# A clock for SyncE's queue in the planner, and the ends of six HGRN heads turned by 32x32 blocks

## The chip, the core and the metric

The kernel runs on one core of one Trainium2 chip. The core's engines are TensorE (PE in the rows, with its weight loads as PEld), VectorE (DVE), ScalarE (ACT), GpSimd (POOL) and SyncE (SP), which issues nearly all DMAs. The metric is the device time of one execution in microseconds (us), the median of several runs.

## The reference, cut to what matters

One layer of a streaming encoder over 512 frames of 2048 features in float32. One input projection feeds two groups of heads, their gated outputs go through one output projection, and the result is normalised with the residual:

```
proj = x @ w_in                          # 512 x 2048 by 2048 x 8320
o_rwkv = rwkv7(proj[:4224]) * silu(z_r)  # 16 heads of 64: scan over chunks of 64 frames
o_hgrn = hgrn2(proj[4224:]) * silu(z_h)  # 8 heads of 128: gated linear recurrence, RMS norm
y = concat(o_rwkv, o_hgrn) @ w_out       # 512 x 2048 by 2048 x 2048
out = layer_norm(2 ** 0.25 * x + y)
```

What the change touches is the end of an HGRN head: its output of 512 frames by 128 values is divided by its root mean square over the values, and multiplied by a weight for each value and by silu(z):

```
o = o * rsqrt(mean(o * o, -1) + 1e-5)
o = o * g_norm_w * silu(z)
```

## The kernel before, in words

**Tiles.** Activations lie with 128 features on the partitions and 512 frames along the row. Each float32 product of the two projections is made of three products of halves (`xh`, `xl` of the activations, `wh`, `wl` of the weights, in the type float32r); the helper `three` issues them. Weights come in pieces of 128x1024 (`wr`, two buffers, 512 KB each, helper `load`), and each piece is split in two parts of 512 columns by ScalarE (`wh`, three buffers) and VectorE (`wl`, three buffers). A part feeds 12 products.

**Order of the work.** The input projection is a list of units of 128 columns (`_order`), 48 products each, which write one of four PSUM banks `main`. Between those products a planner (class `Plan`) puts everything else: for four groups of two pairs of RWKV heads the preparation (`rwkv_prep`), the inversion and the scan (`rwkv_invert`, `rwkv_scan`), the finish (`rwkv_finish`); for four groups of two HGRN heads `hgrn_heads`, which ends in `hgrn_out` for each head. These are generators in queues. The planner has a clock for each engine, a cost for each operation, and for each tile the times at which it is ready and free. After each product of a projection it goes round the queues and issues what its clocks allow: an operation for TensorE only when its inputs are ready 0.35 us ahead of TensorE's clock (`LEAD`), one for another engine when it would start soon (`SLACK`, `EARLY`). So the costs and due times in the planner decide the order in which instructions stand on each engine; on the chip each engine works its list through in order and waits on semaphores.

**Modes of TensorE.** The planner tells three kinds of product apart: *main* (float32r, 512 columns), *whole* (float32, 128x128) and *narrow* (fewer than 128 rows or columns). In what follows a *visit* is a run of whole or narrow products between two main ones.

**Turning a tile.** A head's values come out of its products with frames on the partitions, but the gated output `g` needs values on the partitions. In `hgrn_out` four products with the identity matrix (helper `tr`, one for each 128 frames) turn `o2` into a PSUM tile `pn`, which VectorE then multiplies with the weight and `S["g"]` (helper `stt`, into `g`). A second way exists already in the helper `turned`, which `rwkv_prep` uses for `bk` and `v`: VectorE turns each 32x32 block in place (`dtr`), and 16 DMAs (8 for `v`) from SBUF to SBUF, all from SyncE, carry the blocks to where they belong. In `turned` the planner holds 0.4 us for each DMA of a row of blocks, and takes the result as ready 3 us after the last hold.

**SyncE's queue.** Weights, the finished outputs `g` that are put away to DRAM and brought back (`spill`), the residual and the result are all issued from SyncE, in order. The planner before has a clock for DMA transfers (`fetched`) that starts from TensorE's clock; time that SyncE needs to issue is not in it. The finishes of RWKV pairs stand in one queue, `finishes`, one after the other.

**The out projection.** After the last unit its 16 inputs (`korder`: pairs 0 to 5, heads 0 to 5, then head 6, pair 6, head 7, pair 7) are split as the weights are, one step ahead of use, by `split_gated`. For the first quarter of the columns the 16 inputs are used in that order, 12 products each.

Of the kernel before, what the change touches and what calls it, by code (L numbers as in the profile page):

```python
# [15 lines left out]
P = 128  # L16
T = 512
D = 2048
# [44 lines left out]
class Plan:  # L63
# [15 lines left out]
    def __init__(self, room):  # L79
        self.clock = {"pe": 0.0, "dve": 0.0, "act": 0.0, "pool": 0.0, "dma": 0.0}  # L80
# [65 lines left out]
    def fetched(self, tile, size):  # L146

        self.clock["dma"] = max(self.clock["dma"], self.clock["pe"]) + size * 128 / 360e3
        self.ready[tile.tensor.name] = (self.clock["dma"] + 2.0, "dma")
# [92 lines left out]
def mixer_kernel(ctx, tc, head, x_r, w_all, par, up, ln_wb, consts, hmask, out):  # L242
# [64 lines left out]


# [83 lines left out]
    def turned(dst, src, tmp, rows=4, base=0):  # L392


        name = dst.tensor.name
        yield dtr(tmp, src)
        yield lambda: by_now(tmp)
        for a in range(4):
            for b in range(rows):
                o = base + 32 * b  # L400
                nc.sync.dma_start(dst[o : o + 32, :, 32 * a : 32 * a + 32],
                                  tmp[32 * a : 32 * a + 32, :, 32 * b : 32 * b + 32])
            at = plan.clock["pe"] + 0.4 * rows
            yield lambda: plan.clock["pe"] >= at
        plan.ready[name] = (plan.clock["pe"] + 3.0, "dma")
# [21 lines left out]
    def load(j):  # L427
        if j < nload:
            raws[j] = st("wr", [P, HALF])
            nc.sync.dma_start(raws[j], w_all[j - nhead])  # L430
# [117 lines left out]
    def constants():  # L548
        raw = st("ksq", [P, T])[:, : 16 * len(LEVELS)]
        for t, a in ((pr, par), (cst, consts), (raw, hmask)):  # L550
            nc.sync.dma_start(t, a)
# [48 lines left out]
    def put_gated(k, g):  # L600

        gated[k] = g
        if k in SPILL:
            def run():
                yield lambda: by_now(g)
                nc.sync.dma_start(spill[SPILL.index(k)], g)
# [8 lines left out]
    def next_up():  # L615
        if len(ups) < NPAIR:
            upw = take("up", [P, 2, P])
            nc.sync.dma_start(upw, up[len(ups)])
# [311 lines left out]
    def rwkv_group(SS, grp):  # L930
# [4 lines left out]
        def run():  # L935
# [3 lines left out]
            for i, S in enumerate(SS):  # L939
                plan.add(finishes, rwkv_finish(S, 2 * grp + i))  # L940
# [116 lines left out]
    def hgrn_out(S, h, q, k, dt_, dg, tot, tots):  # L1057
# [38 lines left out]
        yield landed(o2)  # L1096
        pn = take("mix")
        for j in range(4):
            yield tr(pn[:, j * P : j * P + P], o2[:, j * P : j * P + P])
        yield has(S, "g")  # L1100
        yield stt(g, pn, hcol(HHW, h), S["g"], ALU.mult, ALU.mult)
        drop(S["g"], pn, o2)
# [30 lines left out]
    groups, finishes, preps = plan.queue(), plan.queue(), plan.queue()  # L1133
# [14 lines left out]
    def fetch(k):  # L1148
        raw = firsts[k] = take("q4", [P, T + FIRST * P])
        if k:  # L1150
            nc.sync.dma_start(raw, head[k])
        else:

            nc.scalar.dma_start(raw[:, T:], head[k, :, T:])
            for c in (slice(0, T // 2), slice(T // 2, T)):
                nc.sync.dma_start(raw[:, c], head[k, :, c])
# [91 lines left out]
    def reload(n):  # L1248
        while len(asked) < min(n, KT):
            k = korder[len(asked)]  # L1250
            asked.append(k)
            if k in SPILL:
                plan.until(lambda: gated[k] is not None and (plan.free("t") or plan.free("g")))
                gated[k] = take("t" if plan.free("t") else "g")
                nc.sync.dma_start(gated[k], spill[SPILL.index(k)])
# [105 lines left out]
    def finish(t):  # L1361
# [4 lines left out]
        def norm():  # L1366
            ahead = []
            for d in range(5):
# [5 lines left out]
                if d:  # L1374
                    y, b, o, k = ahead.pop(0)
                    yield keyed(tt(y, y, b, ALU.add), k, k)
                    nc.sync.dma_start(o, y)
# [9 lines left out]
    def finish_last(t, pbs, weigh):  # L1387
# [16 lines left out]
        def norm():  # L1404
# [8 lines left out]
            for d in range(4):  # L1413
# [3 lines left out]
                for c in (slice(0, T),) if d < 3 else (slice(0, T // 2), slice(T // 2, T)):  # L1417
# [7 lines left out]
                    nc.sync.dma_start(o[:, c], y[:, c])  # L1425
# [27 lines left out]
    def residual(t, d):  # L1453
        plan.until(room(g=1))
        xrs[t] = take("g")
        nc.sync.dma_start(xrs[t], x_r[t, :, d * T : d * T + T])
# [9 lines left out]
    def ahead(j, d):  # L1466

        if d == 0:
            split_gated(j + 2)
            if j == 8:  # L1470
                plan.until(room(big=1))
                lnw.append(take("big", [P, 2, D]))
                nc.sync.dma_start(lnw[0], ln_wb[None].to_broadcast([P, 2, D]))
# [193 lines left out]
```

## Time and profile before

| | us |
|---|---|
| median of 3 runs (1050.09 to 1050.93) | 1050.35 |
| the profiled execution | 1050.24 |
| its span in the profile, first instruction to last | 1048.5 |

The profiled execution's own time and its span differ by 1.7 us, which lie outside the instructions. A difference in span is taken as a difference in time. The clock granted to TensorE over the span is 0.999 of full speed, that is the 2.4 GHz level.

### The profile page before, as it was taken

What the parts mean: (1) busy time and instruction counts of PE and PEld (TensorE: products, weight loads), DVE (VectorE), ACT (ScalarE), POOL (GpSimd) and SP (SyncE); (2) the same over time, 40 slices, a digit from 0 to 9 for tenths busy, and PEclk for the clock granted to TensorE, in tenths of its full rate; (3) what the DMA queues carried; (4) which work ended last, traced back from release to release, by engine and by line L of the source; (5) the groups of instructions that cost most, each with busy time, mean ns of one, the idle gap of its engine ahead of it and who ended that gap; (6) DMA issues with size and microseconds to landing.
All of it is one profiled execution on the core that took longest, in us unless ns stands there. A gap on an engine that the chain in (4) does not pass through costs nothing.

```text
span 1048.5 us, 18840 instructions
## 1 busy us (share of the span) xinstructions
PE 1040.6 (99%) x7342; PEld 865.1 (83%) x7342; DVE 755.7 (72%) x1653; ACT 437.6 (42%) x867; POOL 38.3 (4%) x81
## 2 busy tenths in 40 slices
PE   9999999999999999999999999999999999999997
PEld 8888888888888888888888888888888888888885
DVE  7465898667759987676689866865998778625556
ACT  6545333445353354452533353525334554323321
POOL 0000000000000000000000000000000002000000
PEclk9999999999999999999999999999999999999999
DMA  8134342222343522223534323234352244545613
GB/s 332 54 103 114 99 109 86 86 79 81 84 123 100 122 82 74 78 98 79 138 78 118 98 62 96 70 96 110 100 128 72 69 164 131 182 131 159 202 60 131
DMA packets 87305, 114.79 MB, mean 109 GB/s; under 512 B 56368, under 2 KB 58160, under 8 KB 87088
## 3 DMA queue, kind: packets, MB, share of 16 engines
q1 hardware_dynamic: 87072, 113.39, 36.6%
q8 instruction: 58, 0.95, 0.4%
q14 instruction: 31, 0.25, 0.1%
q10 hardware_dynamic: 144, 0.20, 0.1%
HBM read 99.92 MB, written 7.34 MB: 102 GB/s over the span
## 4 chain that ended last, share of the span: by engine, by line
PE 99%; DVE 1%; DVEq 0%; issue 0%
PE main L453 74%; PE mix L324 11%; PE mix L453 8%; PE main L1192 3%; PE main L324 2%; PE mix L328 1%; PE mix L1142 0%; DVE inv L356 0%; DVE inv L347 0%; DVE stats L1549 0%; DVEq L1663 0%; DVE mv L1357 0%; DVE bd L356 0%; DVE mv L352 0%; DVE inv L1140 0%
## 5 line engine op out<-in xcount | busy, mean ns | idle before, releaser
L453 PE MATMUL main<-xl,wh 128*128 128x512 f32 x864 | 341.1, 395 | 0.0
L453 PE MATMUL main<-xh,wl 128*128 128x512 f32 x864 | 341.1, 395 | 0.0
L453 PE MATMUL main<-xh,wh 128*128 128x512 f32 x864 | 340.9, 395 | 0.0
L337 ACT ACTIVATE wh<-wr 128x512 fp32r<-128x512 f32 x299 | 186.9, 627 | 237.1 <-PE main L453 180.5
L347 DVE TENSOR_TENSOR wl<-wr,wh 128x512 fp32r<-128x512 f32 x299 | 203.8, 682 | 61.8 <-ACT wh L337 60.1
L453 PEld LDWEIGHTS main<-xh,wh 128*128 128x128 f32 x864 | 162.4, 188 | 33.0
L453 PEld LDWEIGHTS main<-xh,wl 128*128 128x128 f32 x864 | 162.5, 188 | 32.6
L453 PEld LDWEIGHTS main<-xl,wh 128*128 128x128 f32 x864 | 162.4, 188 | 32.6
L453 PE MATMUL main<-wl,xh 128*128 128x512 f32 (+1 forms) x262 | 102.6, 392 | 0.0
L453 PE MATMUL main<-wh,xh 128*128 128x512 f32 (+1 forms) x262 | 102.1, 390 | 0.0
L453 PE MATMUL main<-wh,xl 128*128 128x512 f32 (+1 forms) x262 | 101.6, 388 | 0.0
L453 PEld LDWEIGHTS main<-wh,xh 128*128 128x128 f32 x262 | 49.2, 188 | 9.9
L453 PEld LDWEIGHTS main<-wh,xl 128*128 128x128 f32 x262 | 49.2, 188 | 9.7
L453 PEld LDWEIGHTS main<-wl,xh 128*128 128x128 f32 x262 | 49.2, 188 | 9.6
L338 ACT ACTIVATE t<-main,om 128x512 f32<-128x512 f32 x33 | 22.4, 687 | 51.1 <-PE main L453 41.6
L356 DVE SCALAR_TENSOR_TENSOR t<-main,pr,t 128x511 f32<-128x511 f32 x33 | 24.4, 747 | 26.5 <-ACT t L338 26.2
L347 DVE TENSOR_TENSOR inv<-inv,inv 64x30 f32<-64x30 f32 (+14 forms) x120 | 38.6, 322 | 2.9
L347 DVE TENSOR_TENSOR inv<-inv 64x30 f32<-64x30 f32 (+14 forms) x120 | 38.4, 320 | 2.3
L347 DVE TENSOR_TENSOR t<-t,tot 128x256 f32<-128x256 f32 x96 | 37.8, 414 | 1.8 <-PE mix L324 1.7
L356 DVE SCALAR_TENSOR_TENSOR bd<-mix,pc,bd 64x64 f32<-64x64 f32 x112 | 31.7, 283 | 7.5 <-PE mix L324 5.2
L337 ACT ACTIVATE zz<-mix 64x64 f32<-64x64 f32 x63 | 13.8, 220 | 46.9 <-PE mix L324 45.8
L338 ACT ACTIVATE t<-main 128x512 f32<-128x512 f32 x32 | 18.5, 598 | 30.7 <-PE main L453 30.2
(222 smaller groups left out, 1328.0 us busy)
## 6 DMA issues: line engine op xcount, KB each, us to landing
wr<-w_all SPq DMA_DIRECT2D x156, 512.0 KB, 3.6
q<-head SPq DMA_DIRECT2D x15, 448.0 KB, 5.9
q<-q SPq DMA_DIRECT2D x128, 32.0 KB, 2.4
g<-x_r SPq DMA_DIRECT2D x16, 256.0 KB, 3.8
spill<-g SPq DMA_DIRECT2D x12, 256.0 KB, 2.7
out<-q SPq DMA_DIRECT2D x12, 256.0 KB, 2.4
t<-spill SPq DMA_DIRECT2D x10, 256.0 KB, 4.2
zz<-ksq SPq DMA_DIRECT2D x64, 32.0 KB, 2.6
```

The lines of the kernel that those rows point to most:

```text
L324: return Op([("pe", cost, lambda: pe.matmul(o, l, r, start=start, stop=stop, **kw))], [l, r], [o], mode="narrow" if narrow else "main" if ...
L328: return Op([("pe", 0.11, lambda: pe.transpose(o, i, ident))], [i], [o])
L337: return "act", cost, lambda: sc_e.activation(o, i, f, scale=scale)
L338: return "act", cost, lambda: sc_e.activation(o, i, f, scale=scale, bias=bias)
L347: return dve_op([a, b], o, lambda: dve.tensor_tensor(o, a, b, f), base=0.16 if o.shape[0] < P and size(o) == C and o.tensor.name in tags e ...
L356: return dve_op([a, b], o, lambda: dve.scalar_tensor_tensor(o, a, s, b, f1, f2), per=0.00113, base=0.085 if o.shape[0] == P else 0.25 if s ...
L453: pe.matmul(ps, l, r, start=first and i == 0, stop=last and i == 2)
L1192: pe.matmul(pss[a], *ops, start=k == 0 and low == of == 0, stop=k == KT - 1 and low == 1)
```

## The change

The planner gets a clock `sp` for SyncE's queue. A new helper `send` issues a DMA and moves that clock on by 0.44 us, or by the cost given; all DMAs from SyncE go through it now. `fetched` starts a transfer from this clock and takes it as landed 1.8 us after its end, where it was 2.0. `turned` no longer holds 0.4 us for each block: it sends a block (0.65 us each) when SyncE's clock is at most 0.2 us ahead of TensorE's, and takes the tile as ready 2.6 us after the last one; it also keeps the source tile busy until then. In `hgrn_out` heads 0 to 5 use `turned` in place of the four products `tr`; heads 6 and 7 keep them. The multiplication that follows then reads `o2` in SBUF where it read `pn` in PSUM. The finishes of the two pairs of a group stand in two queues, not in one.

```diff
@@ -77,7 +77,7 @@
     EARLY = 0.5
 
     def __init__(self, room):
-        self.clock = {"pe": 0.0, "dve": 0.0, "act": 0.0, "pool": 0.0, "dma": 0.0}
+        self.clock = {"pe": 0.0, "dve": 0.0, "act": 0.0, "pool": 0.0, "sp": 0.0, "dma": 0.0}
         self.table = None
         self.mode, self.rest = "main", 0.0
         self.queues, self.waiting, self.hurry = [], {}, False
@@ -145,8 +145,8 @@
 
     def fetched(self, tile, size):
 
-        self.clock["dma"] = max(self.clock["dma"], self.clock["pe"]) + size * 128 / 360e3
-        self.ready[tile.tensor.name] = (self.clock["dma"] + 2.0, "dma")
+        self.clock["dma"] = max(self.clock["dma"], self.clock["sp"]) + size * 128 / 360e3
+        self.ready[tile.tensor.name] = (self.clock["dma"] + 1.8, "dma")
 
     def queue(self):
         self.queues.append([])
@@ -305,6 +305,11 @@
 
         return test
 
+    def send(o, i, cost=0.44):
+
+        nc.sync.dma_start(o, i)
+        plan.clock["sp"] = max(plan.clock["sp"], plan.clock["pe"]) + cost
+
 
     def size(ap):
         n = 1
@@ -397,12 +402,11 @@
         yield lambda: by_now(tmp)
         for a in range(4):
             for b in range(rows):
+                yield lambda: plan.clock["sp"] <= plan.clock["pe"] + 0.2
                 o = base + 32 * b
-                nc.sync.dma_start(dst[o : o + 32, :, 32 * a : 32 * a + 32],
-                                  tmp[32 * a : 32 * a + 32, :, 32 * b : 32 * b + 32])
-            at = plan.clock["pe"] + 0.4 * rows
-            yield lambda: plan.clock["pe"] >= at
-        plan.ready[name] = (plan.clock["pe"] + 3.0, "dma")
+                send(dst[o : o + 32, :, 32 * a : 32 * a + 32],
+                     tmp[32 * a : 32 * a + 32, :, 32 * b : 32 * b + 32], 0.65)
+        plan.ready[name] = plan.busy[tmp.tensor.name] = (plan.clock["sp"] + 2.6, "dma")
@@ -427,7 +431,7 @@
     def load(j):
         if j < nload:
             raws[j] = st("wr", [P, HALF])
-            nc.sync.dma_start(raws[j], w_all[j - nhead])
+            send(raws[j], w_all[j - nhead])
             plan.fetched(raws[j], 4 * HALF)
 
     whole_parts = set()
...
@@ -937,7 +941,7 @@
             yield from outputs(SS, sc)
             drop(sc)
             for i, S in enumerate(SS):
-                plan.add(finishes, rwkv_finish(S, 2 * grp + i))
+                plan.add(finishes[i], rwkv_finish(S, 2 * grp + i))
 
         plan.add(scans[0], run())
@@ -1093,13 +1097,19 @@
         yield tt(tiles(o2), tiles(po), rs[:, :, None].to_broadcast([P, 4, P]))
         drop(po, k, dt_, rs)
         S["used"]()
-        yield landed(o2)
-        pn = take("mix")
-        for j in range(4):
-            yield tr(pn[:, j * P : j * P + P], o2[:, j * P : j * P + P])
+        if h < 6:
+            yield from turned(tiles(o2), tiles(o2), tiles(g))
+            pn = o2
+        else:
+            yield landed(o2)
+            pn = take("mix")
+            for j in range(4):
+                yield tr(pn[:, j * P : j * P + P], o2[:, j * P : j * P + P])
         yield has(S, "g")
         yield stt(g, pn, hcol(HHW, h), S["g"], ALU.mult, ALU.mult)
-        drop(S["g"], pn, o2)
+        if h >= 6:
+            drop(pn)
+        drop(S["g"], o2)
         put_gated(8 + h, g)
 
     def silu2(ps, put):
@@ -1130,7 +1140,7 @@
 
 
     scans = [plan.queue(), plan.queue()]
-    groups, finishes, preps = plan.queue(), plan.queue(), plan.queue()
+    groups, finishes, preps = plan.queue(), [plan.queue(), plan.queue()], plan.queue()
     heads, stores = plan.queue(), plan.queue()
...
```

In the rest of the diff, from `constants` and `put_gated` to the loads at the end, `nc.sync.dma_start(o, i)` becomes `send(o, i)` and nothing else.

What this does to the order of instructions is read from the built programs. In all, TensorE has the same products as before but for 24 `tr` fewer, VectorE has six STREAM_TRANSPOSE of 128x512 more, and SyncE has 96 DMAs of 32x4x32 more. The lists are the same up to product 354 of TensorE (of 5697), and again for the last 626 products of TensorE, the last 133 operations of VectorE and the last 70 DMAs of SyncE; in between everything is shifted. TensorE leaves the main products 31 times for narrow ones, where it was 30, and has 117 runs of whole products, where it was 119.

First place, TensorE at the end of HGRN head 0 (`t_971` is its `o2`, `t_1292` the next head's `k`; `zz`, `q` belong to the RWKV scan). Before:

```order
L453 MATMUL main_2152<-xl_91,wh_2130 128x512
L328 MATMUL mix_2199<-cst,t_971 128x128 x4
L328 MATMUL mix_2209<-cst,t_1292 128x128 x3
L324 MATMUL mix_2214<-zz_832,q_447 128x128
L324 MATMUL mix_2215<-zz_1231,q_885 128x128
L453 MATMUL main_2152<-xh_75,wl_2131 128x512
```

Now, at the next head's `k` (`t_1259`); head 0's own four products are nowhere on TensorE:

```order
L457 MATMUL main_2397<-xh_74,wl_2375 128x512
L333 MATMUL mix_2443<-cst,t_1259 128x128 x3
L329 MATMUL mix_2457<-ksq_2418,ones_r 128x512
L329 MATMUL mix_2457<-ksq_2419,ones_r 128x512
L457 MATMUL main_2397<-xh_75,wh_2374 128x512
```

The four products of `o2` are gone from a visit that stays, with other neighbours. The six sets of four that go all stood, as here, in a visit with other whole products.

Second place, SyncE and VectorE for the same head. SyncE before, from the piece of weights ahead of head 0's spill:

```order
L430 DMA wr_2189<-w_all 128x1024
L606 DMA spill<-g_2080 128x512
L430 DMA wr_2277<-w_all 128x1024
L430 DMA wr_2356<-w_all 128x1024
L618 DMA up_2367<-up 128x256
```

SyncE now (`t_954` is head 0's `o2`, `g_2150` its `g`):

```order
L310 DMA wr_2297<-w_all 128x1024
L310 DMA up_2306<-up 128x256
L310 DMA t_954<-g_2150 32x4x32 x11
L310 DMA wr_2379<-w_all 128x1024
L310 DMA t_954<-g_2150 32x4x32 x5
L310 DMA wr_2451<-w_all 128x1024
L310 DMA spill<-g_2150 128x512
```

The 16 blocks stand between pieces of weights, with one piece amid them. In the other five heads the blocks stand 9 and 7, 6 and 10, 4 and 10 and 2, 11 and 5, 9 and 7 around such pieces. VectorE now, from the multiplication that makes `g` (the 23rd row after the block transposes of `t_954`):

```order
L371 STREAM_TRANSPOSE g_2150<-t_954 128x512
...
L361 SCALAR_TENSOR_TENSOR bd_1985<-mix_2411,pc_1040,bd_1985 64x64
L361 SCALAR_TENSOR_TENSOR g_2150<-t_954,half,t_2084 128x512
L352 TENSOR_TENSOR wl_2445<-wr_2297,wh_2444 128x512
L357 TENSOR_SCALAR ksq_2460<-mix_2457 128x512
L361 SCALAR_TENSOR_TENSOR rt_1986<-mix_2463,zz_872 64x128
L361 SCALAR_TENSOR_TENSOR rt_1987<-mix_2470,zz_1315 64x128
```

The multiplication now waits for 16 DMAs rather than for TensorE, and a split of weights (`wl`) and the next step of the scan (`rt`) stand behind it.

Third place, VectorE at the last input of the out projection, the finish of RWKV pair 7 (`mix_9487` and `mix_9368` hold its turned output). Before:

```order
L356 SCALAR_TENSOR_TENSOR g_9348<-mix_9368,half,t_7437 128x512
L356 SCALAR_TENSOR_TENSOR t_8898<-ksq_9349,t_8898 128x512
L356 SCALAR_TENSOR_TENSOR g_9348<-g_9348,half,t_8898 128x512
L347 TENSOR_TENSOR wl_9383<-wr_9273,wh_9382 128x512
L347 TENSOR_TENSOR xl_9395<-g_9227,xh_9394 128x512
L347 TENSOR_TENSOR wl_9407<-wr_9323,wh_9406 128x512
L347 TENSOR_TENSOR xl_9417<-g_9155,xh_9416 128x512
L347 TENSOR_TENSOR wl_9429<-wr_9323,wh_9428 128x512
L347 TENSOR_TENSOR xl_9441<-g_9348,xh_9440 128x512
```

Now:

```order
L361 SCALAR_TENSOR_TENSOR g_9467<-mix_9487,half,t_7489 128x512
L361 SCALAR_TENSOR_TENSOR t_8945<-ksq_9468,t_8945 128x512
L352 TENSOR_TENSOR wl_9500<-wr_9385,wh_9499 128x512
L361 SCALAR_TENSOR_TENSOR g_9467<-g_9467,half,t_8945 128x512
L352 TENSOR_TENSOR xl_9513<-g_9467,xh_9512 128x512
```

The finish has moved towards its use: on TensorE 47 main products stood between the four `tr` of pair 7 and the first product that reads its split, and now 22 do.

## Rows read from the trace of the kernel before

**Rows 1.** The page: busy time by engine, and the granted clock in 40 slices.
```profile
PE 1040.6 (99%) x7342; PEld 865.1 (83%) x7342; DVE 755.7 (72%) x1653; ACT 437.6 (42%) x867; POOL 38.3 (4%) x81
...
PEclk9999999999999999999999999999999999999999
```

**Rows 2.** All waits of PE: engine, line, releaser, us in total, times, longest.
```profile
PE mix L324 <- ACT ksq L1409: 1.5, 1, 1.5
PE mix L1142 <- DVE inv L1140: 1.1, 1, 1.1
PE mix L324 <- DVE bd L356: 0.4, 1, 0.4
```

**Rows 3.** Timeline of PE, a visit with seven `tr`: start us, us, instruction, count.
```profile
206.70 0.39 PE L453 MATMUL main<-xl,wh 128*128 128x512 f32 x1
206.93 0.93 PE L328 MATMUL mix<-cst,t 128*128 128x128 f32 x7
207.69 0.61 PE L324 MATMUL mix<-zz,q 128*128 128x128 f32 x4
208.06 0.48 PE L453 MATMUL main<-xh,wl 128*128 128x512 f32 x1
208.38 0.39 PE L453 MATMUL main<-xh,wh 128*128 128x512 f32 x1
208.61 0.39 PE L453 MATMUL main<-xl,wh 128*128 128x512 f32 x1
```

**Rows 4.** Groups by line: all `tr`, with busy us and mean ns of one.
```profile
L328 PE MATMUL mix<-cst,t 128*128 128x128 f32 x88 | 12.9, 273 | 0.0
```

**Rows 5.** Timeline of PE, around a visit of narrow products.
```profile
156.85 0.39 PE L453 MATMUL main<-wh,xh 128*128 128x512 f32 x1
157.17 0.70 PE L324 MATMUL mix<-t 128*32 128x16 f32 x62
...
158.37 0.50 PE L453 MATMUL main<-wl,xh 128*128 128x512 f32 x1
158.71 0.39 PE L453 MATMUL main<-wh,xl 128*128 128x512 f32 x1
```

**Rows 6.** Timeline of SyncE's queue, six blocks of `turned` one after the other.
```profile
130.44 3.86 SPq L401 DMA_DIRECT2D zz<-ksq  x6
```

**Rows 7.** Line L401, the blocks of `turned`: ns min/median/max to issue, us from issue to landing.
```profile
L401 SPq DMA_DIRECT2D q<-q x128: 585/608/1292, 74.9 to 768.5; - x128
...
DMA to landing us min/median/max: 1.9/2.5/4.8
```

**Rows 8.** Groups by line: VectorE's block transposes of one 128x512 tile.
```profile
L366 DVE STREAM_TRANSPOSE ksq<-t 128x512 f32<-128x512 f32 x8 | 5.6, 701 | 0.0
```

**Rows 9.** Timeline of all engines at a burst of spill loads, idle time in brackets.
```profile
837.32 1.81 SPq L1255 DMA_DIRECT2D t<-spill  x4
...
841.54 0.63 ACT L337 ACTIVATE xh<-t 128x512 fp32r<-128x512 f32 x1 [2.81 <-DMA t<-spill]
...
842.21 0.69 DVE L347 TENSOR_TENSOR xl<-t,xh 128x512 fp32r<-128x512 f32 x1 [1.76 <-ACT xh L337]
...
845.38 0.39 PE L453 MATMUL main<-xh,wh 128*128 128x512 f32 x1
...
846.03 0.29 DVE L356 SCALAR_TENSOR_TENSOR bd<-mix,pc,bd 64x64 f32<-64x64 f32 x1
...
846.93 0.39 PE L453 MATMUL main<-xh,wl 128*128 128x512 f32 x1
```

**Rows 10.** Timeline of PE and VectorE after the four `tr` of pair 6.
```profile
880.58 0.48 PE L453 MATMUL main<-wh,xl 128*128 128x512 f32 x1
...
880.87 0.75 DVE L356 SCALAR_TENSOR_TENSOR g<-mix,half,t 128x512 f32<-128x512 f32 x1 [1.35 <-PE mix L328]
881.53 0.68 DVE L356 SCALAR_TENSOR_TENSOR t<-ksq,t 128x512 f32<-128x512 f32 x1
882.13 0.68 DVE L360 TENSOR_REDUCE rs<-t 128x4 f32<-128x512 f32 x1
```

More of the change, by code (lines that the diff above doesn't have):

```diff
@@ L550, in constants @@
         for t, a in ((pr, par), (cst, consts), (raw, hmask)):
-            nc.sync.dma_start(t, a)
+            send(t, a)
             plan.fetched(t, 4 * size(t))
@@ L605, in run @@
                 yield lambda: by_now(g)
-                nc.sync.dma_start(spill[SPILL.index(k)], g)
+                send(spill[SPILL.index(k)], g)
                 drop(g)
@@ L617, in next_up @@
             upw = take("up", [P, 2, P])
-            nc.sync.dma_start(upw, up[len(ups)])
+            send(upw, up[len(ups)])
             plan.fetched(upw, 8 * P)
@@ L1150, in fetch @@
         if k:
-            nc.sync.dma_start(raw, head[k])
+            send(raw, head[k])
         else:
@@ L1155, in fetch @@
             for c in (slice(0, T // 2), slice(T // 2, T)):
-                nc.sync.dma_start(raw[:, c], head[k, :, c])
+                send(raw[:, c], head[k, :, c])
         plan.fetched(raw, 4 * size(raw))
@@ L1254, in reload @@
                 gated[k] = take("t" if plan.free("t") else "g")
-                nc.sync.dma_start(gated[k], spill[SPILL.index(k)])
+                send(gated[k], spill[SPILL.index(k)])
                 plan.fetched(gated[k], 4 * T)
@@ L1376, in norm @@
                     yield keyed(tt(y, y, b, ALU.add), k, k)
-                    nc.sync.dma_start(o, y)
+                    send(o, y)
         plan.add(norms, norm())
@@ L1424, in norm @@
                                     kc + k_r + [p.tensor.name], kc)
-                    nc.sync.dma_start(o[:, c], y[:, c])
+                    send(o[:, c], y[:, c])
         plan.add(norms, norm())
@@ L1455, in residual @@
         xrs[t] = take("g")
-        nc.sync.dma_start(xrs[t], x_r[t, :, d * T : d * T + T])
+        send(xrs[t], x_r[t, :, d * T : d * T + T])
         plan.fetched(xrs[t], 4 * T)
@@ L1472, in ahead @@
                 lnw.append(take("big", [P, 2, D]))
-                nc.sync.dma_start(lnw[0], ln_wb[None].to_broadcast([P, 2, D]))
+                send(lnw[0], ln_wb[None].to_broadcast([P, 2, D]))
                 plan.fetched(lnw[0], 8 * D)
```

## Prediction

> **What bounds the kernel now.** The page first: TensorE is busy 1040.6 us of the span, VectorE 755.7, and the granted clock is at its upper level in every slice [rows 1]. Busy time alone proves little, since pipelined products overlap in the rows; so the waits come next. All waits of TensorE together are 3.0 us: 1.1 before the first products, 1.5 near the end, and 0.4 at a step of the scan [rows 2]. The timeline then shows that main products follow each other at 0.23 us whatever stands between them [rows 3]. So the kernel is a list of products worked through at their own pace, and time is won or lost in three ways only: fewer products, cheaper changes of mode, or a wait that appears or goes. The last 626 products and all that follows them on the other engines stand in the same order as before, so the 1.5 us wait and the end stay; I take them at no change.
>
> **The 24 products that go.** Between the first of seven `tr` (206.93) and the next product (207.69) lie 0.76 us [rows 3], 0.109 us each. All six sets of four stood beside other whole products, so their visits stay and each `tr` gives back just its pitch: 24 x 0.109 = 2.6 us. A lower bound is the mean over the whole visit, (208.06 - 206.93) / 11 records = 0.103, or 2.5 us; an upper one the busy time of all 88, 12.9 / 88 = 0.147 [rows 4], or 3.5 us. I take 2.6, since the products that follow a `tr` start by its pitch.
>
> The mean duration of one `tr` is 273 ns [rows 4], more than twice its pitch. The Trainium skill, "TensorE: Matmul & The Clock Gate", Part 4: PE-mode transpose, gives about 275 ns for a 128x128 transpose in one kernel; the row agrees as a duration. By that page 24 of them would be 6.6 us, against 2.6 by the pitch. The Trainium skill, "VectorE: DVE Perf Modes", Rules for kernel authors, speaks against the edit: a full 128x128 transpose belongs on TensorE if PSUM will do as its destination, and here it did; no row here tests that.
>
> **Changes of mode.** One narrow visit more. Entering one costs 157.17 - 156.85 - 0.23 = 0.09 us over the pitch and the first main product after it 158.71 - 158.37 - 0.23 = 0.11 [rows 5]: 0.2 us. Two runs of whole products fewer: the first main product after one is 208.38 - 208.06 - 0.23 = 0.09 late [rows 3], so they give at most 0.18. But two places where a narrow run went straight into a whole one are gone too, which takes some of that back; I take nothing here and keep 0.18 as a bound.
>
> **VectorE.** Six block transposes of 128x512 at 701 ns [rows 8] are 4.2 us more, spread over six heads; the multiplication that follows is one operation as before. VectorE is idle 1048.5 - 755.7 = 293 us, so this costs nothing unless it stands ahead of something that TensorE is about to need, where it costs up to 0.7.
>
> **SyncE.** Six blocks of the kind that exists take 3.86 us, the last one 0.61 of it: (3.86 - 0.61) / 5 = 0.65 us from one to the next [rows 6, 7]. The new ones carry half as much; at the same price 96 are 62 us of a queue that else waits most of its time for buffers of weights to come free. The planner before held 0.4 us for each, so 16 blocks ran 16 x 0.25 = 4 us behind its plan, and the weights behind them too; now it holds 0.65, and a piece of weights stands behind at most one block. TensorE lost nothing to the old lag [rows 2], so I take nothing for its going, and nothing for the new blocks.
>
> **The new wait.** The multiplication on VectorE waits for 16 blocks, and behind it stand a split of weights and the scan's next `rt`, which TensorE wants. The planner takes the last block as ready 0.65 + 2.6 = 3.25 us after its issue; the old blocks landed 2.5 us after it in the median, 4.8 at worst [rows 7]. So a stop on VectorE lies between nothing and 1.55 us a head. I take nothing: the median lies well below the planned time, and in five of six heads the last block is five or more behind a piece of weights.
>
> **The clock itself.** One wait of before is of the kind that this clock should see. Five spill loads go out from 837.32; ScalarE gets the first at 841.54, after 2.81 us idle, VectorE then waits 1.76, the scan's `bd` ends 846.32 and TensorE's visit is late [rows 9]. From the visit's planned start (845.38 + 0.23) to the second main product are 1.32 us, where a visit of the same kind takes 208.38 - 207.69 = 0.69 [rows 3]: 0.63 us lost. The old plan had that load ready after 0.73 + 2.0 = 2.73 us, the new one after 0.44 + 0.73 + 1.8 = 2.97; on the chip it took 4.2. So the new clock moves this by a quarter of a microsecond, and I take no gain; 0.63 is the bound. All times but the chip's in this step are constants of the code.
>
> **Sum.** -2.6 + 0.2 = -2.4 us. The profiled execution is 1050.24 (span 1048.5), which is 0.11 below the median of the runs; on it 1047.8, a span of 1046.1, and for the median 1050.35 - 2.4 = 1047.9. A change of 0.2%, 2.1 us here, is about what a measurement of this kernel can tell from none; the forecast lies just 0.3 us beyond it.
>
> **Rival 1, the gain is eaten by waits (no measurable change).** The likeliest place is the last finish. Count from the first main product after pair 7's `tr`. By pair 6's rows VectorE starts 0.29 us later, and then its operations follow at 0.66 and 0.60 [rows 10]. Now the chain is: multiplication 0.66, second one 0.60, a split of weights 0.60, the last one 0.75 (ends 2.9), ScalarE's copy 0.63 and VectorE's difference 0.69 [rows 9], some 4.4 with hand-overs of 0.1. TensorE reads the copy after 22 products (22 x 0.23 + 0.09 = 5.1) and the difference after 24 (5.6). So 1.2 us are left, where 25 more products (5.7 us) were left before. Each microsecond that VectorE is late here beyond 1.2 is one of TensorE, and no rule of the planner holds a product back for these splits. Between the outputs of the last scan and this finish VectorE has little slack, since two finishes now run side by side with the splits. With 0.3 to 4.5 us lost in such places the result is within 0.2%; 1 us lost gives 1048.9.
>
> **Rival 2, slower: the six multiplications hold VectorE up.** If each block lands as late as the worst of before, VectorE stops 1.55 us; the planner lets TensorE take a result 0.35 us after it is due, so up to 1.2 us reach TensorE at each head, 6 x 1.2 = 7.2 us: 1050.35 - 2.4 + 7.2 = 1055.1. It decides from 4.5 us in all, 0.75 a head. For it: the operations behind are those of the scan, which TensorE takes soonest. Against it: in rows 9 a stop of 2.81 us on ScalarE cost TensorE 0.63, about a fifth. At that rate six stops of 1.55 would cost 2.1 us, which is rival 1 again.
>
> **Rival 3, a `tr` is worth its duration.** 24 x 0.273 = 6.6 us, 1050.35 - 6.6 + 0.2 = 1043.9. That is what the figure of the page on TensorE would make of it. Against it: the product after seven `tr` starts 0.76 us after the first, not 1.9 [rows 3].
>
> That the change doesn't do what it says can be left aside: the 24 products are not in TensorE's list any more.
>
> **How the numbers follow.** Forecast 0.53, rival 1 0.33, rival 2 0.11, rival 3 0.03. The forecast's own range is 1047.1 (all of 0.63 and 0.18 regained) to 1048.2 (0.3 us of new waits). The range asked for starts at 1047.0, which leaves rival 3 out, and reaches to 1051.0, which takes in rival 1 up to 3 us lost and leaves out most of rival 2. Faster by over 0.2%: forecast and rival 3, 0.56; within 0.2%: 0.33; slower: 0.11.
>
> **What the profile after would show.** Right: 64 `tr` at 0.11 us in visits, TensorE's waits again some 3 us in all, main products at 0.23, a span near 1046.1. Rival 1: new rows among TensorE's waits with VectorE or ScalarE as releaser, above all in the last finishes, after some 880 us [rows 10]. Rival 2: VectorE's multiplication into `g` from `t` with idle time before it ended by a DMA, and waits of TensorE on `rt` or `bd` soon after. Wrong in another way: weights that land late (ScalarE's `wh` waiting longer for `wr` and TensorE then for `wl`), or a wait for a PSUM bank, since tiles of heads are now held some 13 us longer (16 x 0.65 + 2.5) and evacuations ask for free tiles; no row before prices that.

## The result, and the profile after

| kernel | median, us | lowest to highest (runs) |
|---|---|---|
| before | 1050.91 | 1050.09 to 1051.34 (17) |
| changed | 1052.45 | 1050.68 to 1055.69 (17) |

The ratio of the changed kernel to the one before is 1.0016, 95% interval 1.0010 to 1.0023: 1.5 us more, where 2.4 us less was forecast. The interval leaves 1 out, so the change made the kernel slower, though by less than the 0.2% that the prediction took as the least measurable change; 1052.45 lies above its range (1047.0 to 1051.0). Of the distance to the forecast of 1047.9, 0.56 us is the kernel before itself, whose median was 1050.35 when the forecast was made. The changed kernel scatters over 5.0 us, the one before over 1.25. The mean granted clock goes with it: the eight of its runs at 0.999 or 1.000 take 1050.7 to 1052.5 us, the nine at 0.996 to 0.998 take 1052.3 to 1055.7. The profiled execution of the changed kernel took 1053.0 us (span 1051.2, clock 0.997); that of before, 1050.24 (span 1048.5).

The page of the changed kernel, its first rows and the queue of TensorE's instructions (packets, MB, share of 16 engines):
```profile
span 1051.2 us, 18939 instructions
...
PE 1039.9 (99%) x7318; PEld 863.5 (82%) x7318; DVE 754.1 (72%) x1644; ACT 444.7 (42%) x884; POOL 40.1 (4%) x81
...
q8 instruction: 58, 0.95, 0.4%
```
Against [rows 1] 24 products are gone (7342 to 7318), and busy time has hardly moved: the busy rows don't say where 2.7 us of span have gone.

All waits of TensorE, as in [rows 2], and the group of the remaining `tr`, as in [rows 4]:
```profile
PE mix L329 <- issue: 2.6, 2, 1.5
PE mix L329 <- ACT ksq L1419: 1.5, 1, 1.5
PE mix L1152 <- DVE inv L1150: 1.1, 1, 1.1
PE mix L333 <- DVE t L352: 0.8, 1, 0.8
PE main L1202 <- ACT t L342: 0.3, 1, 0.3
```
```profile
L333 PE MATMUL mix<-cst,t 128*128 128x128 f32 x64 | 9.9, 272 | 0.8 <-DVE t L352 0.8
```
64 `tr` are left, of the same duration. Three rows are new: 0.3 us at the first products, 0.8 for VectorE ahead of a `tr`, and 2.6 us in two places in narrow products with "issue" behind the arrow, which means that TensorE waited for nothing that a semaphore shows.

Timeline of TensorE around the first of the two, in a visit of narrow products (start us, us, instruction, count, idle time before it):
```profile
607.65 0.70 PE L329 MATMUL mix<-t 128*32 128x16 f32 x62
...
608.22 0.70 PE L329 MATMUL mix<-t,t 128*32 128x16 f32 x62
608.85 0.37 PE L329 MATMUL mix<-big,inv 32*32 32x32 f32 x18
610.68 0.59 PE L329 MATMUL mix<-big,inv 32*32 32x32 f32 x46 [1.47 <-issue]
611.20 0.50 PE L457 MATMUL main<-xh,wh 128*128 128x512 f32 x1
```
The same place in stretches (length, busy us of TensorE, its weight loads, VectorE, ScalarE, GpSimd, then the granted clock, DMA share, GB/s):
```profile
609.25:610.68 1.43, 0.00 (x0) 0.00 (x0) 1.27 (x7) 0.00 (x0) 0.00 (x0) 1.00 0.00 0
610.68:612.00 1.32, 1.32 (x49) 1.15 (x49) 0.81 (x5) 0.66 (x2) 0.00 (x0) 0.99 0.05 12
612.00:615.30 3.30, 3.30 (x9) 2.63 (x8) 1.36 (x3) 1.87 (x6) 0.00 (x0) 0.50 0.01 2
615.30:620.00 4.70, 4.70 (x25) 3.94 (x25) 2.94 (x11) 2.93 (x8) 0.00 (x0) 0.99 0.37 110
```
In the middle of a group of equal products TensorE stops for 1.6 us, and the profile shows no semaphore that it waits for. From 612.0 to 615.3 the granted clock is 0.50, the 1.2 GHz level: eight main products follow each other at 0.427 us instead of 0.227, 1.6 us more. The second stop and the wait ahead of pair 7's `tr`:
```profile
821.62 0.57 PE L329 MATMUL mix<-t,t 128*32 128x16 f32 x46
823.30 0.32 PE L329 MATMUL mix<-t,t 128*32 128x16 f32 x16 [1.11 <-issue]
...
894.95 0.63 PE L333 MATMUL mix<-cst,t 128*128 128x128 f32 x4 [0.84 <-DVE t L352]
```
Beyond the usual pitches, the second stop is 1.24 us and the wait 0.99; 0.7 us go at the first products (7.0 to 9.7 us).

**Where the time went.** If from the starts of TensorE's instructions all gaps of more than 0.06 us over the usual pitch are taken out, what is left of the list is 2.3 us shorter in the trace after than in the trace before (2.4 was forecast), and the gaps are 5.0 us more. New are 1.60 + 1.24 (stops), 1.58 (clock), 0.99 (pair 7) and 0.71 (start), 6.1 in all; gone are 0.54 at the spill burst [rows 9] and some 0.6 of smaller ones. -2.3 + 5.0 is the 2.7 us by which the span grew. Some tenths hang on what is called usual: with the median pitch of each two shapes, tiles or modes that follow each other, the list is 2.5 to 2.8 us shorter and the gaps are larger by as much more.

**What the stops are.** TensorE's 14,822 records (products, their weight loads, waits) come in 58 packets of 16 KB, so 256 to a packet, that is some 128 product records with their loads. (A `tr` or a main product is one product record; any other float32 product of the program is two, as the 51 tiny products of a1 below make 102.) The two stops lie 3072 records apart, just 12 packets, and both where a packet ends. A packet of main products lasts TensorE 29 us; one of dense narrow products, 10 ns apart, 1.2 us. In the records of that queue the packet behind the first stop starts at 608.0 us, 0.2 us after the packet ahead of it has begun to be worked on, takes 1.35 us, and TensorE goes on 1.34 us after it has landed; at the second, 820.83 us, 1.11 us and 1.37 us. The order of before never puts more than 128 narrow product records that are that dense into one visit; the new order twice puts 192 into one (`t`, `t,t` and `big,inv`, after the 748th and the 2316th main product), so that, wherever packets end, three quarters of a packet or more lie in one of them. The first stop stands in such a visit. The second stands in a visit of 128, of which the order before has many: with another place of the packets' ends, that order stops in one too (b3 below).

The Trainium skill, "Runtime: NRT & Kernel Launch", Instruction fetch mechanics, says that instructions are refilled in blocks of 16 KiB, 256 instructions, and that this is hidden since an engine dispatches more slowly than the blocks are filled. The size agrees with the 58 packets; that it is hidden does not: here the stops cost 1.60 and 1.24 us.

### The profile page after: what moved, and what is told of

Same layout as the page of the kernel before. It is cut to its first block, busy times and chain, and to the rows that moved or that the text cites. A ratio compares the mean times of both kernels' runs of the same rounds, so it can differ in the third digit from the quotient of the medians.

```text
span 1051.2 us, 18939 instructions
## 1 busy us (share of the span) xinstructions
PE 1039.9 (99%) x7318; PEld 863.5 (82%) x7318; DVE 754.1 (72%) x1644; ACT 444.7 (42%) x884; POOL 40.1 (4%) x81
## 4 chain that ended last, share of the span: by engine, by line
PE 97%; DVE 1%; DMA 1%; issue 0%; POOL 0%; SPq 0%; ACT 0%; DVEq 0%
PE main L457 73%; PE mix L329 11%; PE mix L457 8%; PE main L1202 3%; PE main L329 2%; PE mix L333 1%; DMA q<-head 1%; DVE inv L361 0%; POOL sm L384 0%; DVE sm L365 0%; DVE t L352 0%; SPq L310 0%; DVE inv L352 0%; DVE wl L352 0%; ACT xh L342 0%
## 5 line engine op out<-in xcount | busy, mean ns | idle before, releaser
L342 ACT ACTIVATE zz<-mix 64x64 f32<-64x64 f32 x78 | 17.1, 220 | 45.5 <-PE mix L329 44.4
```

The lines of the kernel that those rows point to most:

```text
L342: return "act", cost, lambda: sc_e.activation(o, i, f, scale=scale)
```

## The experiments

Three theories were written down for the first runs. **Theory 1:** the loss is stops at the ends of packets and the clock behind them. **Theory 2:** it is the 96 transfers and the waits on them. **Theory 3:** it is the order that the new planner makes, the two queues of finishes and the last finish above all. Each kernel was timed beside the kernel before, on the same chip.

| label | median, us (lowest to highest, runs) | before there | ratio, 95% interval |
|---|---|---|---|
| a1_after_shifted | 1055.49 (1054.24 to 1057.32, 5) | 1050.63 | 1.0046, 1.0034 to 1.0059 |
| a2_before_shifted | 1056.10 (1055.64 to 1057.34, 5) | 1050.63 | 1.0054, 1.0041 to 1.0066 |
| a3_turned_only | 1060.62 (1058.61 to 1060.86, 4) | 1050.63 | 1.0090, 1.0074 to 1.0105 |
| a4_apart | 1049.46 (1049.37 to 1050.18, 11) | 1050.63 | 0.9991, 0.9982 to 0.9999 |
| b1_after_shift144 | 1051.51 (1049.71 to 1051.91, 11) | 1050.55 | 1.0006, 0.9997 to 1.0014 |
| b2_after_shift228 | 1054.50 (1052.07 to 1057.04, 5) | 1050.55 | 1.0039, 1.0025 to 1.0052 |
| b3_before_shift144 | 1051.97 (1051.47 to 1052.76, 11) | 1050.55 | 1.0013, 1.0004 to 1.0022 |
| b4_all_tr | 1050.76 (1049.72 to 1052.68, 11) | 1050.55 | 1.0002, 0.9994 to 1.0011 |
| c1_apart_all_tr | 1051.79 (1051.09 to 1052.22, 11) | 1050.66 | 1.0010, 1.0001 to 1.0018 |
| c2_one_queue | 1086.11 (1085.45 to 1090.86, 6) | 1050.66 | 1.0334, 1.0320 to 1.0349 |
| c3_after_again | 1051.85 (1050.27 to 1054.48, 11) | 1050.66 | 1.0013, 1.0004 to 1.0022 |
| c4_apart_8_heads | 1075.08 (1073.98 to 1076.32, 4) | 1050.66 | 1.0232, 1.0218 to 1.0246 |
| d1_limit_rest3 | 1054.73 (1053.81 to 1055.47, 5) | 1050.78 | 1.0037, 1.0024 to 1.0049 |
| d2_limit_only | 1048.04 (1047.42 to 1048.35, 8) | 1050.78 | 0.9974, 0.9963 to 0.9984 |

**The instruction stream moved, the order kept (a1, a2).**
```diff
-    WARM, T0 = 9, 4.2
+    WARM, SHIFT, T0 = 6, 51, 4.2       # a2: before, SHIFT 63
+    for _ in range(SHIFT):
+        pe.matmul(warm[:32, :32], zero[:32, :32], zero[:32, :32])
```


> The changed kernel with nothing moved but TensorE's instruction stream: 51 tiny products on the zero tile stand at the program's start, where TensorE waits for its first operands, in place of three of the nine warm-up products, so that every later instruction lies 192 places further back in the packets of 256. Theory 1 (instructions): TensorE stops where a whole packet holds dense narrow products, because it is through before the next one is there; then it also loses the clock once. By pitches the three shortest packets of the changed kernel take 1.25, 1.31 and 1.76 us; with the shift they take 1.83 and 2.40 us, all others above 4. With a stop of about 2.6 us less the packet's own time this falls from 3.5 us to 1.0. Expected: 2 to 4 us faster than the changed kernel, 1048.5 to 1050.5, no stop above 1.2 us without a releaser, the granted clock at 1.00. Theory 2 (the 96 new transfers and the waits on them) and theory 3 (the new order of the scan and the last finish): the order is the same, so 1052.4 +- 0.7 and the same stops after the same products.

> The kernel before with its instruction stream shifted by 240 places in the same way (63 tiny products on the zero tile for three warm-up products), nothing else. Theory 1 (instructions): two packets become short, 1.33 us after the 1568th main product (some 410 us) and 1.76 us after the 2212th (some 581 us); by pitches the stops are about 2.1 us together, where the kernel before has 0.2. Expected: 1052.5 to 1054.5, with stops of TensorE without a releaser at these two places, perhaps a drop of the clock behind one. Theories 2 and 3: nothing that they name has changed, 1050.9 +- 0.5.

Both missed their numbers, first for a reason of their own: the 102 records of a1's tiny products took 5.57 us (55 ns each, where the kernel's own take 11), so its main products began near 9.2 us and a2's at 10.5, against 4.9 us before. Less these 4.4 and 5.6 us, an estimate, they stand at 1051.1 and 1050.5. a2 has no stop, so the two short packets reckoned for it did no harm. In a1 the stops have moved: there is none at the products where the second one was, one of 0.67 is new at 191.2 us, and the one in the visit after the 2316th main product comes 32 product records later, at 614.4 us (2.1, with the clock at 0.50 from 618 to 621). The order is that of the changed kernel, and the places are again ends of packets. That speaks against theories 2 and 3, which expected the same stops at the same products.

**The turned heads with the old planner (a3).**
```diff
-        yield landed(o2)
-        pn = take("mix")
...
+        if h < 6:
+            yield from turned(tiles(o2), tiles(o2), tiles(g))
+            pn = o2
```


> The kernel before, with the six heads' ends turned by VectorE and 96 transfers, but with the old planner: no clock for SyncE, the old pace of the transfers, one queue of finishes. Theory 1 (instructions): no packet is shorter than 2.4 us by pitches, so nothing is lost there and the 24 products that go count: 1048.3 to 1049.3. Theory 2 (transfers and the waits on them): the same loss as with the change, 1051.5 to 1053. Theory 3 (the new order): the last finish is the old one, so 1048.3 to 1049.3 as well; this run does not tell 1 from 3.

10 us slower than before, more than any theory had. The long waits of VectorE for transfers, and TensorE's:
```profile
DVE g L356 <- DMA t<-g: 10.8, 5, 3.1
...
DVE ksq L347 <- DMA zz<-ksq: 7.1, 1, 7.1
```
```profile
PE mix L324 <- DVE ksq L347: 6.1, 1, 6.1
...
PE mix L324 <- issue: 1.1, 1, 1.1
```
Blocks of a head and blocks of `zz` take turns on SyncE's queue, each planned at 0.4 us and taking 0.65; VectorE stops for 7.1 us, TensorE for 6.1 of them, and ten main products behind it run at 1.2 GHz. The row with "issue" is a stop at the end of a packet, at 825 us, where theory 1 had expected none. With the queue's clock and two queues of finishes, in the changed kernel, VectorE's wait for the blocks `t<-g` is 0.2 us in all. Theory 2 names a real cost, which half of the change makes and the other half takes away again.

**Narrow groups kept apart (a4).**
```diff
-    REST = 1.5
+    REST = 4.0
...
+        if op.mode == "narrow" == self.mode and self.dense >= 64:
+            return False
```
(`dense` counts the narrow products of the visit.)

> The changed kernel with two numbers of the planner: a narrow visit of TensorE takes no further narrow product once it holds 64, and 4 us instead of 1.5 pass before the next narrow visit. The three groups of narrow products that stood in one visit stand apart, and the shortest packets take 2.8 and 3.5 us by pitches instead of 1.25 and 1.31. Theory 1 (instructions): no stops without a releaser, no drop of the clock, what is left is the wait at the last finish (about 1 us) and one or two more visits (0.2 each): 1048.5 to 1050.3. Theory 2: the transfers are all there, 1052 +- 1. Theory 3: the two queues of finishes and SyncE's clock are there, 1052 +- 1.

As theory 1 expected: no stop at the end of a packet, no drop of the clock, all eleven runs within 0.81 us, 1049.46. Its order also has 0.16 us of wait at pair 7 instead of 0.99, so the run alone does not say how much is the stops'.

**Shifts again, with quicker tiny products, and their control (b1 to b3).**
```diff
+    for i in range(SHIFT):             # b1, b3: 39; b2: 60
+        q = slice(i % 4 * 32, i % 4 * 32 + 32)
+        pe.matmul(warm[q, :32], zero[q, :32], zero[q, :32])
```


> The changed kernel with its instruction stream 144 places further back; the 39 tiny products that do it now lie on four different quarters of the array, so that they should be about as quick as the kernel's own (some 11 ns) and fit into the time in which TensorE waits for its first operands. Theory 1, as the first six traces mend it: TensorE stops without a releaser where the 160 products (320 instructions) ahead of a packet's end take less than some 4.6 us, because the next packet is asked for about that far ahead. In the changed kernel's trace, stops taken out, the two shortest such stretches are 3.1 and 4.55 us; with this shift the shortest is 4.46. Expected: no stop above 0.5 us, no loss of the clock, and 2.5 to 4 us faster than the changed kernel: 1048.5 to 1050. Theories 2 and 3: 1052.4 +- 0.7.

> The same with 228 places (60 tiny products). Theory 1: the shortest stretches are 1.54 us (ends at the dense visit after the 2316th main product, some 609 us) and 3.08 us (at some 821 us): stops of 3.1 and 1.5 us by 4.6 us less each, perhaps with a drop of the clock behind the long one. Expected: 2 to 5 us slower than the changed kernel, 1054 to 1057. Theories 2 and 3: 1052.4 +- 0.7.

> The kernel before with the same 39 tiny products and the same shift as b1: what the shifting itself costs. By theory 1 no stretch of the kernel before gets shorter than 5.4 us with this shift (and than 4.3 with any shift), so nothing is gained or lost but at the start: 1050.6 +- 0.5. Were it the tiny products or the shorter warm-up that make b1 and b2 quicker or slower, it would show here.

b1 and b3 missed: the rule of 160 products in 4.6 us, drawn from six traces, does not hold. b1 stops for 1.86 us in the other of the two long visits, and b3, the kernel before, at 821.6 us for 0.81, which with some 0.8 more at the first products makes its 1.4 us. TensorE and the stretches in b1:
```profile
187.13 0.37 PE L329 MATMUL mix<-big,inv 32*32 32x32 f32 x19
189.23 0.59 PE L329 MATMUL mix<-big,inv 32*32 32x32 f32 x45 [1.73 <-issue]
```
```profile
187.00:190.00 3.00, 1.27 (x87) 1.09 (x77) 2.38 (x12) 0.14 (x1) 0.00 (x0) 1.00 0.00 0
190.00:193.40 3.40, 3.40 (x9) 2.67 (x9) 1.24 (x3) 2.39 (x7) 0.00 (x0) 0.52 0.03 5
```
The stop, and the low clock with it, have gone from 609 to 187 us, where 39 tiny products at the start moved the end of a packet. The four of b1's eleven runs at a mean clock of 1.000 take 1049.7 to 1051.0 us, the seven at 0.997 or 0.998 take 1051.5 to 1051.9. b2 did what it was to do: a stop of 2.3 us at 610.7 and one of 0.87 at 825.7:
```profile
613.08 0.65 PE L329 MATMUL mix<-big,inv 32*32 32x32 f32 x32 [2.19 <-issue]
```
```profile
613.00:619.50 6.50, 6.42 (x46) 5.10 (x46) 1.58 (x4) 2.53 (x7) 0.00 (x0) 0.50 0.22 78
```
The low clock lasts 6.8 us here. The median of b2 lies 3.0 us above that of b1, which has the same order; 1.4 us of this can be the start, where TensorE in b2's trace reaches its 22nd main product that much later, after a wait of 1.29 us for ScalarE.

**The new planner without turned heads (b4).**
```diff
-        if h < 6:
+        if h < 0:
```


> The changed kernel with all eight heads turned by TensorE as before: the clock for SyncE's queue and the two queues of finishes alone. The 24 products and their visits are back, the 96 transfers are gone. Theory 1: two dense visits stand closer than before (96 narrow products of the program after the 748th main product, 88 after the 2304th), so a stop or none: 1050 to 1052, with any loss at stops without a releaser. Theory 2 (transfers): 1050.5 or a little less. Theory 3 (the order that the new planner makes is worse by itself): 1053 to 1055, with waits for VectorE or ScalarE at the last finish.

1050.76, the same as before within 0.1%: in the trace no stop, and no wait of TensorE but the two at the ends. Its order too puts 192 product records into one visit (after the 748th main product), so a long dense visit does not make a stop by itself; it depends on where in it a packet ends. One of the eleven runs took 1052.68 us at a mean clock of 0.998; there is no trace of it. The clock for SyncE's queue and the two queues cost nothing by themselves; theory 3 falls in that form.

**The worth of the 24 products, one queue, the change again, and eight heads (c1 to c4).** c1 is a4 with `h < 0`, c4 is a4 with `h < 8`, c3 is the changed kernel, and c2 is the changed kernel with
```diff
-                plan.add(finishes[i], rwkv_finish(S, 2 * grp + i))
+                plan.add(finishes, rwkv_finish(S, 2 * grp + i))
```


> The kernel of a4 (narrow groups apart) with all eight heads turned by TensorE: against a4 it prices the 24 products alone, with the stops out of the way in both. By the prediction's step (0.109 us each, 2.6 in all) and its visits (0.2 back): a4 is 2.1 to 2.6 us faster than this kernel, which then takes 1051.5 to 1052.1. If a product saved is worth less than its pitch, or the transfers and waits of the turned heads cost something even with the new planner, the difference is smaller: 0.5 to 1.5 us. This kernel should show no stop without a releaser above 0.5 us.

> The changed kernel with the finishes of a group's two pairs in one queue, as before, and all else as changed. The order then puts three narrow groups, 152 products of the program, directly one behind the other after the 3190th main product (some 815 us), where the changed kernel has 64, and leaves the two visits after the 748th as they are. Theory 1: a stop without a releaser of 1 to 2.3 us near 815 us, most likely with a drop of the clock behind it, in place of the two at 609 and 822 us: 1050 to 1053, with a scatter of more than 2 us between runs. If the two queues were the cause of the loss (theory 3), this kernel would be at 1048 to 1049.

> The changed kernel once more, unchanged, on the chip of c1, c2 and c4. Theory 1: the stops come at the same two products (609 us, in the dense visit after the 2316th main product, and 822 us, after the 3100th) because the packets end there, while their length and the drop of the clock differ from run to run: 1051 to 1054. Theory 3: the wait ahead of pair 7's four products (0.99 us at 893.7) is there as well.

> The kernel of a4 with all eight heads turned by VectorE and transfers. If a product that goes is worth 0.109 us wherever it stands, eight more give 0.9: 1048.3 to 1048.8. Against it: the last two heads end when the last multiplications of the program already wait for their result, and their transfers take some 13 us instead of the four products' 0.5; then TensorE or VectorE waits there, and it takes 1049.5 to 1056.

c1 is 2.33 us slower than a4, inside what was expected, but not cleanly: against expectation it has a stop of 1.5 us at 835.8, again at the end of a packet and in spite of the limit of 64 (the view of waits puts it down to VectorE's `bd`, but that ended 0.7 us before TensorE went on, and the packet landed 1.44 us before), and a4 has two narrow visits more and 1.3 us of smaller gaps that c1 lacks. With all gaps taken out as above, the lists differ by 1.8 us (2.0 to 2.5 by the other pitches).

c2 missed by far. What it shows is not the packet:
```profile
800.00:837.00 37.00, 37.00 (x368) 30.26 (x367) 32.55 (x75) 10.94 (x20) 1.21 (x3) 1.00 0.53 139
837.00:868.00 31.00, 12.98 (x317) 10.62 (x315) 26.02 (x78) 9.80 (x28) 0.00 (x0) 0.59 0.08 26
```
From 837 to 868 us just 4 main products run, where the changed kernel has 98; TensorE waits for ScalarE (10.4 us) and VectorE, step by step through the last scans, at 1.2 GHz for most of it. With one queue, turned heads and SyncE's clock the last scans come when the main products that should cover them are used up. That the shared queue holds them back is argued from the order, not traced further. a3 has one queue as well, with the old planner, and is 25 us quicker: it is the pair of one queue and the new clock that costs this much.

c3 has both stops at the same products (608.6 us, 1.60, and 821.7 us, 0.66), the low clock from 611.9 to 615.3, and 0.99 us at pair 7; nothing at the first products, so the 0.7 us there were that run's.

c4 loses 24 us: VectorE waits 8.4 and 12.0 us for the blocks of the last two heads, and TensorE behind it:
```profile
PE main L460 <- ACT xh L345: 20.9, 2, 13.8
```

**Which of a4's two numbers (d1, d2).** d1 has the limit of 64 and `REST = 3.0`, d2 the limit and the old 1.5.

> The kernel of a4 with 3 us instead of 4 between narrow visits, the limit of 64 narrow products kept. By pitches its shortest packet takes 2.8 us (some 173 us, where the changed kernel has the same one and does not stop) and the next 4.0. Theory 1: no stop without a releaser above 0.5 us and the clock at its upper level throughout: 1048.6 to 1049.8, with a scatter below 1 us. If a4 is quicker for another reason, its longer distance between visits as such, or the last finish alone, this kernel lies between a4 and the changed kernel, 1050 to 1051.5.

> The changed kernel with the limit of 64 narrow products a visit alone, and the old 1.5 us between visits. No visit holds 96 products any more, but by pitches one packet is short, 1.52 us, after the 2221st main product (some 585 us). Theory 1: a stop of 0.5 to 1.5 us there, no drop of the clock or a drop in some runs: 1049.5 to 1051.5. If it were the long visits as such that cost, and not the packet, this kernel would be as quick as a4, 1049.4.

d2 is quicker than expected and the quickest of all: 1048.04. Its waits of TensorE are the two that no order here touches:
```profile
PE mix L332 <- ACT ksq L1422: 1.5, 1, 1.5
PE mix L1155 <- DVE inv L1153: 1.1, 1, 1.1
```
No stop (the packet reckoned short was asked for 4.2 us before the one ahead of it began), the clock at 1.00 until the last product, and no more than 0.09 us lost ahead of any of the last `tr`. d1 has no stop and no drop either, as theory 1 had it, and is nevertheless 4 us slower than before:
```profile
...
PE mix L336 <- DVE t L355: 1.0, 1, 1.0
PE mix L336 <- DVE zz L397: 0.9, 1, 0.9
PE mix L332 <- ACT zz L345: 0.8, 1, 0.8
PE mix L332 <- DVE bd L364: 0.6, 3, 0.2
...
```
All these lie between 877 and 895 us: the last scan and the last finishes. So there are two causes: stops at the ends of packets, which a1, b1 and b2 move while the order, and with it the wait at pair 7, stays; and waits at the end of the scans, which d1 has without any stop. That the latter come with small shifts of the order is argued: `REST` of 1.5 and of 4.0 has none above 0.2 us but the two at the ends (d2, a4), the value between them has these, and why was not traced.

**The stops of all sixteen traces.** Twelve, each at the end of a packet: after (2), a1 (2), a3, b1, b2 (2), b3, c1 and c3 (2). Counted in TensorE's records, eleven of them stand at the same remainder of a division by 256 (192), and b3's one record further. In all twelve TensorE goes on 1.34 to 1.53 us after the packet has landed. At the other ends of packets, more than 800, that time is 1.54 us or more, but for two (1.34 and 1.41) where nothing was lost. The packet ahead of a stop lasted 1.2 to 2.8 us, and the one behind it started 0.1 to 1.6 us after that began.

## Why the prediction was wrong, point by point

- **What bounds the kernel: the step that failed.** "Time is won or lost in three ways only: fewer products, cheaper changes of mode, or a wait that appears or goes." The waits looked at were those with a releaser. There is a fourth way: TensorE has operands and no instructions. It cost 2.8 us in the profiled execution and 2.3 in c3, and 1.6 more by the clock behind the longer stop in each. The trace before had no stop, and I did not look at how dense the visits of the new order are, though the order was there to read.
- **The 24 products: right.** 2.3 us by the lists of the two traces, visits included, or 2.5 to 2.8 by the other pitches (2.4 was forecast); 64 `tr` of unchanged duration are left. d2, which has the same 24 fewer and neither stops nor new waits, is 2.74 us faster than the kernel before beside it (0.26%, 0.16 to 0.37%), 0.3 us more than the forecast. It has another order of the narrow visits as well, so it bears the step out and does not price the 24 alone.
- **Changes of mode: right as a count.** 31 narrow visits (30 before) and 117 whole runs (119). That three narrow groups now share a visit is not in the count, and had no price.
- **VectorE, and the new wait: right.** VectorE's wait for the blocks `t<-g` is 0.2 us in all, taken as nothing; that for TensorE ahead of multiplications into `g` from `mix` is not new. Rival 2 does not happen in the changed kernel; it does where the queue has no clock (a3, 10.8 us on VectorE) or the heads are the last (c4, 8.4 and 12.0 us).
- **SyncE and the clock itself: wrong about its worth.** "I take no gain" and "nothing for its going" were read from the kernel before, with its 192 blocks. For 288 blocks the clock and the second queue together are worth the 8 us between a3 and the changed kernel; the clock without the second queue makes it worse (c2). The stall at the spill burst is gone as well, 0.54 us by the gaps where 0.63 was the bound and nothing was taken; what removed it was not tested.
- **Rival 1: its outcome, for the smaller part by its cause.** It spoke of 0.3 to 4.5 us lost and a result within 0.2%; the medians give 2.4 + 1.5 = 3.9 us lost and 0.16%. That this fits is luck for the larger part, since the stops and the clock are no waits on VectorE or ScalarE. Pair 7's `tr` wait 0.99 us for VectorE in every trace of that order (after, a1, b1, b2, c3). The chain that was priced, the reading of copies behind the finish, did not stop TensorE; the finish itself came late.
- **Rival 3: refuted** by the lists: 2.3 us, not 6.6.

Open stays why the packets are asked for so differently, from 4.8 us before to 7.9 us after the packet ahead begins (to 2.5 us after it in 19 of 20 cases); the rule tried for it (b1, b3) failed, and so did the reckoning of single short packets (a2, d2). Open too is whether the DMA traffic has a part in it: no run changed the traffic and nothing else.

## What to carry to other kernels

Where TensorE runs hundreds of tiny products in a row, count instructions as well as time: keep a dense group to a packet's worth (here 64 products of the program, 128 product records) and put long products between groups; here that one rule in the planner turned a change that lost 1.5 us into one that gains 2.7. The rule alone is no guarantee: it gives another order; d2's happens to be free of late waits too, d1 has the rule and loses 4 us to such waits, and c1 has it and stops for 1.5 us. A scatter between runs that goes with the mean granted clock can point to stops, and a wait whose releaser reads "issue", in the middle of a group of equal instructions, is where to look. Give every queue that work is moved to its own clock in the planner, and look at what shares its order: the same six heads cost 10 us with the old planner, and 35 with the new one and a single queue of finishes.

## What the hardware showed that was not expected

- TensorE's instructions arrive in packets of 256; a stop at a packet's end took 0.7 to 2.3 us, and work went on 1.34 to 1.53 us after the packet had landed.
- Behind the stops of 1.60 us and more (after, c3, b1, a1, b2) the granted clock was 0.50 for 3.4 us, in b2 for 6.8, beginning between 0.3 us before (b2) and 1.6 us after TensorE went on; behind those of 0.66 to 1.5 us (after, c3, b2, b3, a1, a3, c1) it stayed at 1.00. The eight products that ran at 1.2 GHz in the changed kernel cost 1.6 us, as much as the stop.
- Tiny products of 32x32 took 55 ns a record when all used the same 32 rows and wrote the same place (a1), 16 ns when four such places took turns (b1, 78 records in 1.22 us), and 11 ns in the kernel's own groups.
